# One store and pieced weaving of the turned head outputs, priorities for the state sums, and a wide value projection for five pairs

## The chip, the cores and the metric

The kernel runs on one core of a Trainium2 chip. The metric is the time of one execution on the device in microseconds (us); of several runs the median counts. The core has five engines that work side by side and wait for each other by semaphores: TensorE (PE in the profile, its weight loads PEld) multiplies matrices, VectorE (DVE), ScalarE (ACT) and GpSimd (POOL) work element by element, and SyncE (SP) issues transfers (DMA). Each engine works through its own instructions in the order in which they were written down for it. TensorE writes its results to PSUM, a small memory of eight banks; the other engines read them there.

## The reference

It is one layer of a decoder over 1024 tokens of 1024 features: a normalisation, a token mixer with an output projection and a residual, a second normalisation, an MLP with squared ReLU and a residual, and a last normalisation. The mixer has two branches (RG-LRU and HGRN2), merged by gates. The change lies in the HGRN2 branch and in how its result meets the gates:

```python
proj = h @ w_in
xa, ga, q, f, v, g, m_a, m_b = jnp.split(proj, SPLIT_POINTS, axis=-1)
...
o_inter = jnp.einsum('bhtk,bhkv->bhtv', qc * jnp.exp(cum), state)
...
state = jnp.exp(last)[..., None] * state + jnp.einsum('bhsk,bhsv->bhkv', k_to_end, vc)
...
o = rms_norm(hgrn2_chunkwise(qf, kf, log_f, vf), hg_norm)
y_b = o.reshape(B_, S_, HG_HEADS * HG_DV).astype(h.dtype) * jax.nn.silu(g)
y = jax.nn.sigmoid(m_a) * y_a + jax.nn.sigmoid(m_b) * y_b
return y @ w_out
```

`v` is the value projection, `h` times 1024 columns of `w_in`. `state` is carried from chunk to chunk. `o` holds the head outputs, normalised per head. All of it is float32.

## The kernel before

**Number format.** TensorE multiplies numbers of a shortened float32 (fp32r). To keep float32's accuracy, each operand is split into a high part H (ScalarE's cast, L95 or L121) and a low part L (what is left, VectorE, L99), and each product is made three times, H x H, H x L and L x H, summed in one PSUM bank (`mm3`, L155). The parts of a weight tile of 128 x 1024 lie in tiles with the tag `w`, six at a time. Low parts that are needed a second time are stored in memory (`rest`) and loaded again.

**Stages.** The tokens are cut into two halves of 512 (c = 0, 1) and the heads and channels into four pairs (p = 0 to 3), which gives eight pairs of work, i = 4c + p. Stage i projects `xa`, `q` and `f` of pair i and makes its RG-LRU gates (`pr`, `pi`). It begins with the value projection of the pair before it, i - 1 (`v_of`, `v_steps`; for the first pair another function does it). Between these products TensorE makes the HGRN2 products of pair i - 1 (`hgrn`): scores `sc`, transposes of the scaled keys `pk`, the additions to the state `pkv`, the head outputs `po`. The order of TensorE's instructions is written out: `hgrn` calls `go(n)`, which issues n steps of the stage; `pin` keeps that order. The other engines' orders come from a planner, which goes by the place in the program and by priorities (`tc.high_priority`): a higher one puts an instruction further ahead.

**The value projection.** In `v_steps` (L537) the normalised activations are the stationary operand and the weights the moving one, 256 columns at a time. For each of four groups of 128 tokens and each of eight slices of the features, `mm3` makes three products of 256 columns into the first half of a bank. ScalarE then copies 128 x 256 results to the tile `v` (L551).

**The keys, the state and the outputs.** VectorE scales the keys `kk` in several steps (L694 is a helper that records all multiplications). TensorE transposes them (`pk`, L863), ScalarE copies the result to `kT` (L868), TensorE multiplies by `v` (`pkv`, L873), VectorE makes the four states after each other (`sn`, L884), and TensorE makes the outputs (`po`, L898 and L901).

**Turning.** `on_T` (L558) turns the normalised outputs so that channels come first. The transposing DMA works on units of two bytes, so each float32 falls apart into its two halves, which lie in different rows. `stored` writes them to the memory tensor `od` with two transfers, which put the two halves of one channel beside each other.

**The gates.** After the mixer stages come 14 groups of seven products each (`own`, quads 2 to 15; quad = 4 x pair + gate, gates g, mb, ga, ma). `gate_step(q, step)` makes one of the seven products, 12 matmuls of 512 columns, into the bank X, Y or Z (`gX`, `gY`, `gZ`). For steps 0 to 2 ScalarE copies the bank to a tile `ge` (L1209), for steps 3 to 5 VectorE adds it to one (L1212). `gate_work(q)` applies the gate after a group. At gate 1 of a pair, `with_o(p)` (L1278) loads the turned outputs of the pair from `od` (`op`, L1281), lets ScalarE weave the two halves of each float32 together in one copy of 128 x 4096 units of two bytes (`o`, L1282), and multiplies them into the gate on VectorE (L1285). For the first pair this is called by hand at the end of quad 3 (`own[1]`).

**Queues.** Nearly all loads go through SP's queue in the order of the planner. `in_turn` (L1174) chains some of them one behind the other with a high priority: the weights of quads 2, 3 and 4 and the combined activations `t1`, `n2`, `T3`, `T4` (`gT4L` is the last half of them). The stores of the turned outputs go through ScalarE's queue.

After the gates come the output projection, the MLP and the last normalisation. The change does not touch their work; only the tiles of their weight parts are taken through a new helper.

## Time and profile before

| | |
|---|---|
| runs | 1527.86, 1531.04, 1532.47 us |
| median | 1531.04 us |
| the profiled execution, its own time | 1529.59 us |
| its span | 1527.8 us |
| TensorE, VectorE, ScalarE, GpSimd busy | 99%, 75%, 53%, 10% |
| granted clock of TensorE | 0.999 |
| transfers | 311.01 MB, mean 204 GB/s |
| stores of the turned outputs (od) | 16 of 256 KB |
| loads of the turned outputs (op) | 4 of 1024 KB |

How to read the rows that follow: a row of a timeline has the start and the length in us, the engine and the line, the operation, the tile written and the tiles read, the shape and type, the count, and in square brackets how long the engine was idle before and what ended the idle time. A row of a tile's list has the shortest, median and longest duration in ns. A row of the waits names who waited for whom, then the total in us, the number of times and the longest. A row of the chain of waits has the start, the length and the work. A row of the table by stage has the stretch, its length, the busy time of TensorE, its weight loads, VectorE, ScalarE and GpSimd (each with its count of instructions), the granted clock, the share of the transfer engines and GB/s. A matmul's duration in a row contains its way through the array; what it costs in a dense row of them is the distance of two starts.

### The profile page before, as it was taken

Reading aid. Unit: us, or ns where it says so; the run is one execution under the profiler, and the core shown is the slowest. Engines: PE = TensorE matmul, PEld = TensorE weight load, DVE = VectorE, ACT = ScalarE, POOL = GpSimd, SP = SyncE. Lnnn points to the kernel's source line nnn. Section 1 sums busy time; section 2 is a strip of 40 time slices with the busy share of each in tenths; the row PEclk is TensorE's granted clock in tenths of the full one; section 3 lists DMA queues with packets and bytes.
Section 4 is the critical chain, followed back from the end, with each engine's and each line's share of the span. In section 5 each row is a group of like instructions: output and inputs, shape, how many; then the busy total and the mean of one; then the engine's idle time right before and its main releaser. Section 6 shows DMA issues by size and latency. Waiting matters only on the chain.

```text
span 1527.8 us, 23130 instructions
## 1 busy us (share of the span) xinstructions
PE 1514.5 (99%) x9027; PEld 1268.6 (83%) x9027; DVE 1147.3 (75%) x1661; ACT 811.1 (53%) x1333; POOL 154.5 (10%) x191
## 2 busy tenths in 40 slices
PE   9999999999999999999999999999999999999998
PEld 7888988888889878788888888888888888888886
DVE  6888686485585738786856578888888998888877
ACT  6556746656668336555553447666666722111115
POOL 1021110232633600000000000000000000000000
PEclk9999999999999999999999999999999999999999
DMA  8546456476674384332339334666666766666642
GB/s 298 199 170 217 153 198 221 143 230 220 207 240 158 110 311 156 135 137 87 134 106 331 128 111 161 259 248 251 248 250 249 253 264 264 249 249 250 250 191 110
DMA packets 100047, 311.01 MB, mean 204 GB/s; under 512 B 25313, under 2 KB 38753, under 8 KB 87010
## 3 DMA queue, kind: packets, MB, share of 16 engines
q1 hardware_dynamic: 93392, 298.91, 54.0%
q10 hardware_dynamic: 6546, 10.62, 2.0%
q8 instruction: 71, 1.16, 0.3%
q14 instruction: 38, 0.31, 0.1%
HBM read 201.50 MB, written 103.81 MB: 200 GB/s over the span
## 4 chain that ended last, share of the span: by engine, by line
PE 77%; DVE 4%; DMA 2%; ACT 1%; issue 1%; SPq 0%; DVEq 0%; ACTq 0%
PE uX L158 11%; PE dX L158 11%; PE gX L158 8%; PE po L158 6%; PE dY L158 6%; PE uY L158 6%; PE gY L158 4%; PE pj_f L158 3%; PE pv L158 3%; PE pj_q L158 3%; PE pj_xa L158 3%; PE uZ L158 3%; PE dZ L158 3%; PE gZ L158 2%; PE mb L158 1%
## 5 line engine op out<-in xcount | busy, mean ns | idle before, releaser
L1836 DVE TENSOR_TENSOR acc<-acc,dX 128x512 f32<-128x512 f32 x128 | 85.0, 683 | 26.8 <-PE dX L158 26.1
L95 ACT CAST wA<-q 128x512 fp32r<-128x512 f32 x46 | 28.6, 622 | 118.5 <-PE dX L158 94.4
L99 DVE TENSOR_TENSOR wL<-raw,wH 128x1024 fp32r<-128x1024 f32 x46 | 56.3, 1226 | 33.8 <-ACT wH L95 32.9
L158 PE MATMUL po<-wH,y 128*128 128x512 f32 x256 | 80.5, 391 | 0.0
L95 ACT CAST wH<-raw 128x1024 fp32r<-128x1024 f32 x46 | 48.2, 1049 | 35.1 <-DMA raw<-wts_in 14.8
L1736 POOL TENSOR_TENSOR gx<-acc,gain 128x256 f32<-128x256 f32 x1 | 0.7, 741 | 604.6 <-DVE acc L1836 604.6
L158 PEld LDWEIGHTS po<-wH,y 128*128 128x128 f32 x256 | 48.1, 188 | 9.8
L1836 DVE TENSOR_TENSOR acc<-acc,dY 128x512 f32<-128x512 f32 x64 | 43.6, 685 | 14.3 <-PE dY L158 13.8
L158 PE MATMUL po<-wL,y 128*128 128x512 f32 x128 | 49.8, 389 | 0.0
L1584 ACT ACTIVATE b<-b 128x512 f32<-128x512 f32 x48 | 30.0, 625 | 29.7 <-DVE b L1583 27.9
L158 PE MATMUL uX<-h2B11H,wA 128*128 128x512 f32 x128 | 42.1, 390 | 0.0
L193 POOL TENSOR_TENSOR rstd_h<-rstd_h,mhalf 128x1 f32<-128x1 f32 x8 | 4.3, 543 | 373.0 <-DVE rstd_h L188 373.0
L121 ACT CAST wH<-raw 128x1024 fp32r<-128x1024 f32 x36 | 37.2, 1045 | 7.3 <-issue 3.7
L99 DVE TENSOR_TENSOR wA<-q,wA 128x512 fp32r<-128x512 f32 x46 | 31.4, 685 | 12.8 <-ACT wA L95 12.8
L596 DVE SCALAR_TENSOR_TENSOR xc<-xp,pvt,xc 128x512 f32<-128x512 f32 x48 | 40.0, 841 | 1.2 <-ACT xc L580 1.1
L158 PE MATMUL gX<-hT00H,wA 128*128 128x512 f32 x112 | 36.8, 389 | 0.0
L502 POOL TENSOR_TENSOR stt<-r,stt 128x256 fp32r<-128x256 f32 x16 | 21.2, 1344 | 122.4 <-ACT stt L501 110.2
L1121 DVE TENSOR_TENSOR s<-q,q 128x512 f32<-128x512 f32 x46 | 31.6, 687 | 1.4 <-DMA q<-mlp_in 1.1
L1129 DVE TENSOR_TENSOR s<-q 128x512 f32<-128x512 f32 x46 | 31.5, 685 | 0.2
L905 ACT ACTIVATE on<-po 128x128 f32<-128x128 f32 x64 | 16.8, 277 | 26.1 <-PE po L901 26.0
L1585 ACT ACTIVATE b<-b 128x512 f32<-128x512 f32 x48 | 30.1, 630 | 1.0
L158 PEld LDWEIGHTS uX<-h2B11H,wA 128*128 128x128 f32 x128 | 24.0, 188 | 4.9
(2325 smaller groups left out, 5291.2 us busy)
## 6 DMA issues: line engine op xcount, KB each, us to landing
q<-mlp_in SPq DMA_DIRECT2D x92, 512.0 KB, 3.9
raw<-wts_in SPq DMA_DIRECT2D x80, 512.0 KB, 4.7
rest<-wL SPq DMA_DIRECT2D x36, 512.0 KB, 2.9
wL<-rest SPq DMA_DIRECT2D x36, 512.0 KB, 4.1
hd<-ri SPq DMA_DIRECT2D x16, 256.0 KB, 3.0
od<-onT ACTq DMA_DIRECT2D x16, 256.0 KB, 5.9
cdT<-stT SPq DMA_DIRECT2D x16, 256.0 KB, 3.1
op<-od SPq DMA_DIRECT2D x4, 1024.0 KB, 6.7
```

The costliest lines, as they stand in the source:

```text
L95: ins = casts[name] = A.copy(h, src)
L99: ins = V.tensor_tensor(out=lo, in0=src, in1=h.bitcast(F32), op=ALU.subtract)
L121: A.copy(h, raw)
L158: ins = PE.matmul(o, a, b, start=begins, stop=ends, **how)
L502: G.tensor_tensor(out=lo, in0=src, in1=h.bitcast(F32), op=ALU.subtract)
L596: ins = V.scalar_tensor_tensor(xc[:, s, :], xp[:, j : j + T], pvt[:, PV_CW + 8 * j + u : PV_CW + 8 * j + u + 1], xc[:, s, :], op0=ALU.mult ...
L905: A.activation(row(s, n), halves_of(po[s][:, n * P : (n + 1) * P]), AF.Square, accum_out=ssq[:, 4 * s + n : 4 * s + n + 1],)
L1121: ins = V.tensor_tensor(out=sa[:, 0, :], in0=a21, in1=a22, op=ALU.add)
L1129: V.tensor_tensor(out=sb[:, 0, :], in0=a21, in1=a11, op=ALU.add)
L1584: A.activation(b[:, at, :], b[:, at, :], AF.Relu, scale=-1.0 if at == 2 else 1.0)
L1585: A.activation(b[:, at, :], b[:, at, :], AF.Square)
L1836: return V.tensor_tensor(out=dst, in0=dst, in1=banks[bk, pr], op=op)
```

## The change

- The high and low part of a weight tile become two halves of one tile (`w_pair`); three such tiles take the place of six single ones.
- In `v_steps`, for the pairs with i = 2 to 6, one product of 512 columns (H x H beside H x L, into the two halves of a bank) and one of 256 columns (L x H, into the first half) take the place of three products of 256. ScalarE copies the second half of the bank to `v`, and VectorE adds the first half, with a priority of 400.
- The copies to `kT` and the state sums (L868, L882, L884) get a priority of 100.
- `stored` makes one transfer instead of two, and no longer puts the halves beside each other; the load does that now, with two transfers instead of one (`load_o`).
- The weaving copy is cut into four pieces of 512 tokens. For the pairs 1 to 3 (`spread_o`) the pieces come behind the bank copies of steps 0, 1 and 2 of the next quad, the fourth right after the third, and the product with the gate after step 3. For pair 0 the load joins the chain of `in_turn`, behind `T4`; two pieces each come behind the bank copies of steps 1 and 2 of quad 3, and `with_o(0)` keeps its place with the product alone.

```diff
--- before.py
+++ after.py
@@ -110,9 +110,16 @@
         nc.sync.dma_start(raw, seq[i])
         return raw
 
+    both_parts = {}
+
+    def w_pair(pool, name):
+        t = pool.tile([P, 2, 1024], F32R, tag="w", name=name, bufs=3)
+        both_parts[name] = t
+        return t[:, 0, :], t[:, 1, :]
+
     def split_w(i, raw):
         if i < n_mix + 3:
-            h, lo = (wp.tile([P, 1024], F32R, tag="w", name=f"w{q}{i}", bufs=6) for q in "HL")
+            h, lo = w_pair(wp, f"w{i}")
         else:
             h, lo = (kept[0].tile([P, 1024], F32R, tag=f"k{q}{i - n_mix}", name=f"w{q}{i}") for q in "HL")
         at = pair_tiles[i] if i < len(pair_tiles) else None
@@ -383,7 +390,7 @@
         ws, pv = {}, {}
 
         def w_high(i):
-            ws[i] = tuple(wp.tile([P, 1024], F32R, tag="w", name=f"w{q}{i}", bufs=6) for q in "HL")
+            ws[i] = w_pair(wp, f"w{i}")
             keep(A.copy(ws[i][0], xraws[i]))
 
         def w_low(i):
@@ -536,19 +543,29 @@
 
     def v_steps(c, p, got, between):
         v = mt("v", f"v_{c}{p}", (P, 4, 256))
-        w = [next_w(), next_w()]
+        wide = NPAIR * c + p in (2, 3, 4, 5, 6)
+        w = [(both_parts[f"w{used[0]}"], next_w())[0] for _ in range(2)]
         for tt in range(4):
             pp = bank("sc" if tt == 2 else "pj", f"pv_{c}{p}_{tt}")
             for k in range(8):
                 hh, hl = kt(hT[c], k)
                 cut = slice(tt * P, (tt + 1) * P)
                 cols = slice((k % 4) * 256, (k % 4 + 1) * 256)
-                wh, wl = w[k // 4]
-                mm3(pp[:, :256], hh[:, cut], hl[:, cut], wh[:, cols], wl[:, cols], k == 0, k == 7)
+                both = w[k // 4][:, :, cols]
+                if wide:
+                    pin(PE.matmul(pp.rearrange("p (a b) -> p a b", a=2), hh[:, cut], both, start=k == 0, stop=False))
+                    pin(PE.matmul(pp[:, :256], hl[:, cut], both[:, 0, :], start=False, stop=k == 7))
+                else:
+                    mm3(pp[:, :256], hh[:, cut], hl[:, cut], both[:, 0, :], both[:, 1, :], k == 0, k == 7)
                 if k % 2:
                     if k < 7:
                         yield
-            A.copy(v[:, tt, :], pp[:, :256])
+            if wide:
+                A.copy(v[:, tt, :], pp[:, 256:])
+                with tc.high_priority(400):
+                    V.tensor_tensor(out=v[:, tt, :], in0=pp[:, :256], in1=v[:, tt, :], op=ALU.add)
+            else:
+                A.copy(v[:, tt, :], pp[:, :256])
             between(tt)
             yield
         got["v"] = v
@@ -563,10 +580,7 @@
         turned_on.append(ins)
 
         def stored(dma):
-            for g in range(2):
-                dst = od[p][64 * g : 64 * g + 64, :, 2 * c * T : 2 * (c + 1) * T]
-                src = t[:, 8 * g : 8 * g + 8, :].rearrange("p j x -> p (j x)")
-                dma(dst.rearrange("a h t -> (a h) t"), src)
+            dma(od[p][:, :, 2 * c * T : 2 * (c + 1) * T], t.rearrange("p (g j) x -> p g (j x)", g=2))
 
         return stored
 
@@ -865,7 +879,8 @@
         kTs = mt("rr", f"kT{nm}", (P, 2, 4, P))
         for s, u in both:
             kT.append(kTs[:, s])
-            A.copy(kT[s][:, :nkv, :], pk[s][:, : nkv * P].rearrange("p (n k) -> p n k", n=nkv))
+            with tc.high_priority(100):
+                A.copy(kT[s][:, :nkv, :], pk[s][:, : nkv * P].rearrange("p (n k) -> p n k", n=nkv))
         go(at[3])
         pkv = [bank("hg", f"pkv{c}{u}") for _, u in both]
         for s, _ in both:
@@ -878,17 +893,18 @@
             states.append([scar[:, u, :]] + [sn[:, n, :] for n in range(4)])
             for n in range(nkv):
                 kv = pkv[s][:, n * P : (n + 1) * P]
-                if c == 0 and n == 0:
-                    V.tensor_copy(states[s][1], kv)
-                else:
-                    got["states"] = V.scalar_tensor_tensor(
-                        states[s][n + 1],
-                        states[s][n],
-                        t128[:, 4 * s + n : 4 * s + n + 1],
-                        kv,
-                        op0=ALU.mult,
-                        op1=ALU.add,
-                    )
+                with tc.high_priority(100):
+                    if c == 0 and n == 0:
+                        V.tensor_copy(states[s][1], kv)
+                    else:
+                        got["states"] = V.scalar_tensor_tensor(
+                            states[s][n + 1],
+                            states[s][n],
+                            t128[:, 4 * s + n : 4 * s + n + 1],
+                            kv,
+                            op0=ALU.mult,
+                            op1=ALU.add,
+                        )
         go(at[4])
         po = [bank("hg", f"po{c}{u}") for _, u in both]
         for s, u in both:
@@ -1140,7 +1156,7 @@
                     t = pool.tile([P, 2, 1024], F32R, tag=tag, name=f"w{names[0]}{i}", bufs=bufs)
                     h, lo = t[:, 0], t[:, 1]
                 else:
-                    h, lo = (pools[1].tile([P, 1024], F32R, tag="w", name=f"w{names[0]}{i}{q}", bufs=6) for q in "HL")
+                    h, lo = w_pair(pools[1], f"w{names[0]}{i}")
                 ins = split(src(), h, lo, None, lo_behind, (names[0], i))
                 for j, o in enumerate(names):
                     cols = slice(j * 512, (j + 1) * 512)
@@ -1233,7 +1249,7 @@
         elif gate == 1:
             sigmoids(b, b)
             V.tensor_tensor(out=live["g2"], in0=live["g2"], in1=b, op=ALU.mult)
-            with_o(p)
+            spread_o(q, p)
         elif gate == 2:
             t = gp_tile("sg", f"sg{q}")
             A.activation(t, b, AF.Square)
@@ -1275,18 +1291,46 @@
                     for t, y in enumerate((yh, yl)):
                         nc.sync.dma_start(yd[p][:, t, two, :], y[:, two, :].bitcast(F32))
 
-    def with_o(p):
+    woven, due = {}, {}
+
+    def load_o(p, dma):
         parts, o = gp_tile("ld", f"op{p}"), gp_tile("sg", f"o{p}")
         as_16 = lambda t: t.rearrange("p a b -> p (a b)").bitcast(U16)
-        nc.sync.dma_start(as_16(parts), od[p].rearrange("a h t -> a (h t)"))
-        A.copy(
-            as_16(o).rearrange("p (t h) -> p h t", h=2), as_16(parts).rearrange("p (h t) -> p h t", h=2)
-        )
+        for g in range(2):
+            dma(
+                as_16(parts)[64 * g : 64 * g + 64].rearrange("p (h t) -> p h t", h=2),
+                od[p][:, g, :].rearrange("(a h) t -> a h t", h=2),
+            )
+        woven[p] = o
+
+        def piece(j, behind=None):
+            cut = slice(j * T, (j + 1) * T)
+            ins = A.copy(
+                as_16(o).rearrange("p (t h) -> p h t", h=2)[:, :, cut],
+                as_16(parts).rearrange("p (h t) -> p h t", h=2)[:, :, cut],
+            )
+            if behind is not None:
+                held(ins, behind)
+
+        return piece
+
+    def with_o(p):
         ins = V.scalar_tensor_tensor(
-            live["g2"], live["g2"], pvt[:, PV_HG : PV_HG + 1], o, op0=ALU.mult, op1=ALU.mult
+            live["g2"], live["g2"], pvt[:, PV_HG : PV_HG + 1], woven.pop(p), op0=ALU.mult, op1=ALU.mult
         )
         if p == 0:
             behind_steps(ins)
+
+    def spread_o(q, p):
+        piece = load_o(p, nc.sync.dma_start)
+        for j in range(3):
+            due[q + 1, j] = lambda j=j: piece(j, added[q + 1, j])
+
+        def last():
+            piece(3, added[q + 1, 2])
+            with_o(p)
+
+        due[q + 1, 3] = last
 
     yt = {}
 
@@ -1332,6 +1376,7 @@
     gwork[own[0]]["c"]()
     live["g2"] = gp_tile("b", "g2_0")
     nc.sync.dma_start(live["g2"], g2d)
+    piece = load_o(0, in_turn)
     for q in own:
         n = q + 1
         if n > own[1] and n < QUADS:
@@ -1341,6 +1386,11 @@
                 continue
             pinned[0] = q < own[2]
             gate_step(q, step)
+            if (q, step) in due:
+                due.pop((q, step))()
+            if q == own[1] and step in (1, 2):
+                for j in (2 * step - 2, 2 * step - 1):
+                    piece(j, added[q, step])
             if q == own[0] and step == 4:
                 gate_step(own[1], 0)
             if q == own[2] and step == 4:
```

## The prediction

> **What bounds the kernel now.** I read the page first, then a table by stage, then TensorE's own waits, and last the chain of waits.
>
> ```profile
> span 1527.8 us, 23130 instructions
> ...
> PE 1514.5 (99%) x9027; PEld 1268.6 (83%) x9027; DVE 1147.3 (75%) x1661; ACT 811.1 (53%) x1333; POOL 154.5 (10%) x191
> ```
>
> ```profile
> 20.00:545.00 525.00, 524.32 (x4615) 450.40 (x4614) 373.20 (x656) 324.06 (x645) 143.79 (x164) 1.00 0.58 194
> 545.00:645.00 100.00, 97.41 (x426) 79.42 (x425) 68.88 (x75) 51.27 (x61) 0.00 (x0) 1.00 0.56 199
> 645.00:1515.00 870.00, 869.90 (x3868) 720.18 (x3868) 685.66 (x895) 417.02 (x587) 4.32 (x8) 1.00 0.55 208
> ```
>
> ```profile
> PE gX L158 <- ACT ge L1209: 1.4, 2, 1.0
> PE gX L158 <- DMA gT4L<-cdT: 1.2, 1, 1.2
> ```
>
> The second column of the table after the length is TensorE's busy time. TensorE (PE) is the bound from end to end: from 645 us to 1515 us it misses 0.1 us, in the mixer stages (20 to 545) 0.7 us, and only between 545 and 645 a noticeable 2.6 us. So there are two ways to gain: fewer TensorE cycles, or the few stalls. The sum of the stalls that the change can reach is small, which caps the result from the start.
>
> **The change part by part.**
>
> *Value projection.* The chain of waits shows what a product costs when TensorE runs without a break:
>
> ```profile
> 299.40 11.51 PE pv L158 x96
> ...
> 359.70 11.51 PE pv L158 x96
> ...
> 631.33 3.02 PE gX L158 x12
> 634.34 2.72 PE gZ L158 x12
> ```
>
> The first two rows also give the length of a mixer stage, 60.3 us. A product of 256 columns takes 11.51 / 96 = 119.9 ns, one of 512 columns 2.72 / 12 = 226.7 ns. Column for column both stream alike (256 more columns cost 106.8 ns), so each product carries about 13 ns that don't depend on its width. Before, a step of the projection is three narrow products, 359.7 ns. After, it is one wide and one narrow, 346.6 ns. Five pairs with 4 x 8 steps each are 160 steps: 160 x 13.1 ns = 2.1 us less, 0.42 us in each of five stages. The wide operand is two runs of 256 columns with a gap between them, which the trace has not seen at this width. The nearest rows are the small score products, whose operand is contiguous in one and broken up in the other:
>
> ```profile
> L704 PE MATMUL sc<-q,kk x512: 206/206/230, 81.3 to 500.6; 128*32 128x48 f32 x171
> ...
> L704 PE MATMUL sc<-qa,kb x512: 206/206/230, 85.1 to 504.4; 128*32 128x48 f32 x171
> ```
>
> They are equal, so I charge nothing for the gap. The ends are a gain of 2.1 us and, if the wide product cost as much as two narrow ones (239.8 ns), none. The Trainium skill speaks against this term: "TensorE: Matmul & The Clock Gate", in its section on why a gap is 56 ns and not 53.3, gives warm products N / 2.4 GHz plus about 2.5 ns. By that rule a step would go from 327.5 to 325.0 ns and the term would be an estimated 0.4 us. The trace disagrees: 119.9 and 226.7 ns are both some 13 ns above N / 2.4, so the sum goes by the rows.
>
> *What the wide form adds.* VectorE (DVE) now sums the two halves: 4 additions of 128x256 out of PSUM in each stage, 20 in all, each behind ScalarE's (ACT's) copy. These rows of a stage in steady state, by engine, show the price and the cover:
>
> ```profile
> 367.21 0.41 ACT L551 COPY v<-pv 128x256 f32<-128x256 f32 x1
> ...
> 370.47 1.99 ACT L121 CAST wH<-raw 128x1024 fp32r<-128x1024 f32 x2
> ...
> 373.36 0.91 ACT L551 COPY v<-pv 128x256 f32<-128x256 f32 x3
> ```
>
> ```profile
> 382.17 0.42 DVE L694 TENSOR_TENSOR dd<-sc,mf 128x256 f32<-128x256 f32 x1
> ...
> 384.04 0.44 DVE L723 COPY_PREDICATED dd<-mu,sc 128x192 f32<-128x192 uint8 x1 [0.97 <-PE sc L704]
> 384.77 0.75 DVE L596 SCALAR_TENSOR_TENSOR xc<-xp,pvt,xc 128x512 f32<-128x512 f32 x1 [0.29 <-ACT xc L580]
> ...
> 402.52 0.68 DVE L694 TENSOR_TENSOR kk<-kk,seg 128x512 f32<-128x512 f32 x1
> ```
>
> ```profile
> 403.32 0.49 PE L863 MATMUL pk<-ident,kk 128*128 128x128 f32 x3
> ```
>
> An addition like the one at 382.17 (same shape, one operand in PSUM) takes 0.42 us, so a stage gets 1.7 us of VectorE. TensorE reads the values only after pk at 403.32, 30 us later, so they are not late themselves. What is late is the chain behind them: VectorE has 0.97 + 0.29 = 1.26 us of idle time before it makes kk (the keys scaled for the state), and TensorE's transposes take kk 0.12 us after its end (403.20). TensorE also arrives 0.42 us earlier. If all four additions lie in VectorE's busy stretch, pk waits 1.7 - 1.26 + 0.42 - 0.12 = 0.74 us. If they fall into other idle time, it waits nothing. The other stages with a wide projection, by engine:
>
> ```profile
> 217.47 0.89 DVE L694 TENSOR_TENSOR kk<-kk,seg 128x512 f32<-128x512 f32 x1
> ...
> 275.68 0.69 DVE L694 TENSOR_TENSOR kk<-kk,seg 128x512 f32<-128x512 f32 x1 [1.38 <-PE sc L835]
> ...
> 462.14 0.68 DVE L694 TENSOR_TENSOR kk<-kk,seg 128x512 f32<-128x512 f32 x1
> ```
>
> ```profile
> 218.65 0.60 PE L863 MATMUL pk<-ident,kk 128*128 128x128 f32 x4
> 221.41 0.49 PE L873 MATMUL pkv<-v,kT 128*128 128x128 f32 x2 [0.35 <-ACT kT L868]
> ...
> 279.79 0.38 PE L863 MATMUL pk<-ident,kk 128*128 128x128 f32 x2
> ...
> 463.63 0.38 PE L863 MATMUL pk<-ident,kk 128*128 128x128 f32 x2
> ```
>
> ```profile
> 220.77 1.07 ACT L868 COPY kT<-pk 128x512 f32<-128x512 f32 x2
> ```
>
> The stage with pk at 279.79 has 3.4 us to spare and loses nothing. That at 463.63 has 0.81 us and loses at most 0.05. That at 218.65 has 0.29 us and I found no idle time of VectorE to absorb the additions, so up to 1.7 + 0.42 - 0.29 = 1.8 us; but the wait at 221.41 behind it (0.6 with its refill, below) is then already served, which leaves 1.2. With the 0.74 for the stage shown and for the one before it, taken as alike, the give-back lies between 0 and 1.2 + 2 x 0.74 + 0.05 = 2.7 us. I take 1.2, just under the middle, because the additions go to the head of VectorE's order, ahead of the chain that must not be late.
>
> *Priorities of the state's copies and sums.* The wait at 221.41 is one that they aim at: kT's copies start at 220.77, though pk, eight transposes from 218.65 on at 0.15 us or less each, had ended by 219.9. The other is in the second stage:
>
> ```profile
> 108.45 0.46 PE L898 MATMUL po<-v,scT 128*128 128x128 f32 x2 [0.27 <-DVE sn L884]
> ```
>
> A stall costs more than its idle time, since the products after it must refill the pipeline: the 12 products after the wait at 631.33 took 3.02 us against 2.72, and idle time of 1.0 became 1.3. So 0.27 costs about 0.5 and 0.35 about 0.6. Bounds: 0 to 1.1 us gained. I take 0.5 for the first and 0.3 for the second, which the additions may eat. What is put back is the weight casts on ScalarE and the gate's first operations on VectorE, both with idle time after them (ScalarE is busy 324 of 525 us).
>
> *Weaving in pieces.* The turned head outputs are woven on ScalarE in one copy. Rows by engine:
>
> ```profile
> 578.55 4.84 ACT L1282 COPY o<-op 128x4096 uint16<-128x4096 uint16 x1 [2.13 <-DMA op<-od]
> ...
> 593.22 2.01 ACT L1245 ACTIVATE sg<-sg 128x1024 f32<-128x1024 f32 x2 [2.55 <-DVE sg L1243]
> ...
> 622.05 4.83 ACT L1282 COPY o<-op 128x4096 uint16<-128x4096 uint16 x1 [2.29 <-DMA op<-od]
> ```
>
> ```profile
> 580.51 0.69 DVE L1212 TENSOR_TENSOR gb<-gX,ge 128x512 f32<-128x512 f32 x1 [2.03 <-PE gX L158]
> 583.42 2.35 DVE L1285 SCALAR_TENSOR_TENSOR g<-g,pvt,o 128x2048 f32<-128x2048 f32 x1 [2.21 <-ACT o L1282]
> ```
>
> ```profile
> 597.18 0.50 PE L158 MATMUL gX<-gT3H,ws336H 128*128 128x512 f32 x1 [0.38 <-ACT ge L1209]
> ```
>
> The copy at 622.05 holds ScalarE for 4.83 us, the bank copies queue behind it, and TensorE stalls at 631.33: 1.0 idle, 1.3 us in all. In four pieces of about 1.2 us (4.83 / 4, and somewhat more for four starts), each behind a bank copy, with 2.72 us of products between bank copies, nothing queues: 1.3 us gained. I see no reason for less than 1.0. The first copy (578.55) stalls nobody directly, but VectorE waits 2.21 us for it, and its gate work then runs late: ScalarE waits 2.55 us at 593.22 and TensorE 0.38 us at 597.18, 0.65 with its refill. With the outputs loaded ahead, VectorE's product can start behind the addition at 580.51, some 2.2 us earlier than at 583.42. I take the 0.65; its ends are 0 and 0.8. The third and fourth copies stall nobody (0.1 us is missing after 645).
>
> *Stores and loads.* These are off the path:
>
> ```profile
> L569 ACTq DMA_DIRECT2D od<-onT x16: 326/334/446, 126.6 to 546.4; - x16
> ```
>
> ```profile
> 565.26 3.30 SPq L1176 DMA_DIRECT2D q<-mlp_in x2
> ...
> 570.12 0.42 SPq L1281 DMA_DIRECT2D op<-od x1
> ```
>
> ```profile
> 556.07 10.67 DMA gT4L<-cdT
> ```
>
> Eight stores fewer save 8 x 0.33 = 2.7 us of ScalarE's issue time, spread over 400 us in which it has idle time. The loads double in number (4 issues more on SP's queue, 0.3 to 0.4 us each). The first pair moves from 570.12 to just behind the load of gT4L and ahead of the weights issued at 565.26; those weights are for the next group of seven products, 7 x 2.72 = 19 us away. gT4L itself is on the path (TensorE waits 1.2 us for it), so the load must not overtake it: being issued behind it on the same queue, I charge nothing. If the two shared the engines instead, the bound is the transfer of 1 MB at the 199 GB/s of the row 545:645, 5 us. The paired weight tiles free the high part with the low one: at most one product later, 0.12 us, behind two other tile pairs; nothing.
>
> *The sum.* -2.1 + 1.2 - 0.8 - 1.3 - 0.65 = -3.65 us. The profiled execution took 1529.59 us in all, 1.8 us around its span, so it would take 1525.9. It lies 1.45 us under the median of the runs shown, 1531.04, so I forecast **1527.4 us** for the median.
>
> **The rivals.**
>
> *Everything pays in full.* No give-back, both early waits gone: -2.1 - 1.1 - 1.3 - 0.8 = -5.3, 1525.7 us. For it: VectorE is idle for 152 of the 525 us of the mixer stages. Against it: pk's 0.12 us to spare, twice.
>
> *The additions eat the projection.* Give-back 2.7, only the first of the early waits and the 1.3 and 0.65 gained: -2.1 + 2.7 - 0.5 - 1.95 = -1.85, 1529.2 us. For it: the same 0.12 us, and in the stage at 217.47 no gap that I found.
>
> *VectorE blocks on ScalarE: slower.* VectorE works in the order written down for it. The addition has a high priority, the copy it needs has none: ScalarE made three copies only at 373.36, behind the casts at 370.47, while the last values had been ready since 371.21. If the additions stand where the values are ready, VectorE idles about 2.2 us in each stage with the rest of its chain behind it. It decides once the delay exceeds what pk can spare: then 0.74 + 2.2 = 2.9 us in two stages, 2.2 in that of 463.63, 1.2 + 2.2 = 3.4 in that of 218.65, together 11.5; with -2.1 - 0.5 - 1.95 the total is +6.95, 1538.0 us. Against it: the planner that orders both knows of the copy.
>
> *It doesn't do what it says.* The wide product gains nothing, because the fixed 13 ns turn out to belong to the columns of the broken operand: +2.1 on my sum, 1529.5 us. This is near what the rule of the Trainium skill named above would give (an estimate of 1529.1); the row of 119.9 against 226.7 ns speaks against it.
>
> **How the numbers follow.** The likeliest has 0.50, full pay 0.20, eaten 0.17, blocked 0.06, no gain from width 0.05, a head load that overtakes gT4L (+1.3 at its 5 us) 0.02. The repeats of before spread over 4.6 us, which is 0.3%, about what a measurement of this kernel can tell from no change. The likeliest, with its unknowns, spans 1525 to 1530. Faster by over 0.3% means under 1526.4: about a quarter of the likeliest, and 0.6 of full pay: 0.26. Slower by over 0.3%, over 1535.6, is the blocked case and what I overlooked: 0.09. So 0.65 is left for no difference. The range reaches to full pay with a measurement's spread below it, 1523.8, and above past the eaten case to 1532.4; that leaves out the blocked case.
>
> **What would show it.** In the changed profile a narrow and a wide product of pv should follow each other in 347 ns. TensorE's waits should no longer name ge after 620 us nor kT and sn. If the give-back is real, the waits of pk on kk (or of its weight load) appear near 217, 343 and 403 us, in those stages only. If VectorE blocks, its idle time before the additions names v's copy, 2 us at a time. The forecast is wrong if the stage length of 60.3 us falls by less than 0.1 or more than 0.5 us, or if the wait for gT4L grows past 2 us.

## The result, and the profile after

| on one chip, in turns | runs | median, us | lowest to highest |
|---|---|---|---|
| before | 4 | 1529.89 | 1527.86 to 1532.47 |
| after | 4 | 1547.18 | 1543.63 to 1550.33 |

The ratio is 1.0115, with a 95% interval from 1.0097 to 1.0133: the change costs some 17 us. The profiled execution of after took 1543.63 us, the fastest of its four; its span is 14.0 us longer than that of before. The page of after begins:

```profile
span 1541.8 us, 22779 instructions
...
PE 1516.3 (98%) x8867; PEld 1262.1 (82%) x8867; DVE 1148.5 (74%) x1681; ACT 809.7 (53%) x1345; POOL 155.0 (10%) x191
```

There are 160 matmuls less, as the change says, and yet TensorE is busy for 1.8 us more. The table by stage (stretch, length, busy time of TensorE, its weight loads, VectorE, ScalarE, GpSimd, then the granted clock) shows both reasons:

```profile
20.00:545.00 525.00, 524.68 (x4463) 443.21 (x4462) 375.59 (x676) 324.34 (x645) 144.22 (x164) 1.00 0.59 195
545.00:645.00 100.00, 86.52 (x369) 70.68 (x368) 61.05 (x67) 46.46 (x61) 0.00 (x0) 0.93 0.64 172
645.00:1515.00 870.00, 867.94 (x3858) 717.96 (x3857) 679.59 (x876) 410.41 (x577) 4.33 (x8) 1.00 0.55 207
```

Between 545 and 645 us TensorE misses 13.5 us, where it missed 2.6, and its clock is down to 0.93. Between 645 and 1515 it misses 2.1 us, where it missed 0.1. Times between certain products make this exact. In the table, the mixer goes from the first product of `pr` to the first of the gates, the gates to the first of the output projection, and the last column from the first product `dX` of the MLP's second half to the last of the program:

| us | mixer | gates | to the MLP's second half | from there to the end |
|---|---|---|---|---|
| before | 487.60 | 270.35 | 396.32 | 307.96 |
| after | 485.98 | 283.45 | 396.34 | 310.25 |
| difference | -1.62 | +13.10 | 0 | +2.29 |

TensorE's waits in after name who was late:

```profile
PE gX L165 <- ACT ge L1225: 10.5, 1, 10.5
PE gX L165 <- DMA gT4L<-cdT: 2.9, 1, 2.9
...
PE dX L165 <- DVE acc L1886: 1.2, 1, 1.2
PE dZ L165 <- DVE acc L1886: 0.9, 1, 0.9
PE pk L877 <- DVE kk L708: 0.3, 1, 0.3
```

One wait of 10.5 us for `ge`, ScalarE's copy of a gate bank. The chain of waits (start, length, work) tells what it stood behind:

```profile
539.35 20.52 DMA onT<-on
...
569.93 10.45 DMA gT4L<-cdT
```

`onT<-on` is the last turn of the head outputs, a transposing transfer. It takes 20.52 us. These are ScalarE's rows of that time, first of before, then of after, with what each instruction waited for in brackets:

```profile
541.01 1.59 ACTq L561 DMA_TRANSPOSE onT<-on  x1
...
545.70 0.34 ACTq L569 DMA_DIRECT2D od<-onT  x1
```

```profile
559.89 0.55 ACTq L583 DMA_DIRECT2D od<-onT  x1
560.49 0.60 ACT L1060 ACTIVATE smb<-mb 128x512 f32<-128x512 f32 x1 [14.85 <-DMA onT<-on]
...
562.76 0.59 ACT L1225 COPY ge<-gX 128x512 f32<-128x512 f32 x1 [0.73 <-DVE g L1061]
```

The store to `od` stands in ScalarE's queue behind the turn and waits for its data. Before, it was issued 4.7 us after the turn, after the change 20.5 us. The last sigmoid of the mixer (`smb`) and the first `ge` copies stand behind that store, and TensorE behind them. So the question is why the turn became slow. SP's queue, of before and of after, answers it:

```profile
542.53 0.32 SPq L1176 DMA_DIRECT2D gn2L<-cdn  x1
545.59 0.32 SPq L1176 DMA_DIRECT2D gT3H<-cdT  x1
552.86 0.32 SPq L1176 DMA_DIRECT2D gT3L<-cdT  x1
```

```profile
538.36 0.32 SPq L1192 DMA_DIRECT2D gn2L<-cdn  x1
539.86 0.32 SPq L1192 DMA_DIRECT2D gT3H<-cdT  x1
559.89 0.32 SPq L1192 DMA_DIRECT2D gT3L<-cdT  x1
```

Before, the load of `gT3H` (1 MB) was issued at 545.59, just as the turn had landed. After, it was issued half a microsecond behind the turn's issue and moved beside it. The instruction lists of the two programs show why. Each transfer waits on one of eight completion semaphores (DMAHW0 to 7) that are handed out in rotation, so for the transfer eight places ahead of it. Each transfer that lands adds 16 to its semaphore, so the count says which one is meant. The first two lines of each are in SP's list, the third, the store, in ScalarE's:

```
before
221 L1176 DMA gT3H<-cdT_108 128x2048 [waits DMAHW2_49 to 480]
222 L1176 DMA gT3L<-cdT_108 128x2048 [waits DMAHW3_49 to 480]
527 L569 DMA od_100<-onT_6094 128x1024 [waits DMAHW2_49 to 480]
after
221 L1192 DMA gT3H<-cdT_108 128x2048 [waits DMAHW3_49 to 448, DMAHW2_49 to 464]
222 L1192 DMA gT3L<-cdT_108 128x2048 [waits DMAHW3_49 to 464]
518 L583 DMA od_100<-onT_5871 256x1x1024 [waits DMAHW3_49 to 464]
```

What the store waits on is the turn. Before, the turn was on semaphore 2 of the rotation, and `gT3H`, eight places on, had to wait for the same count: until the turn had landed. One store less shifts everything behind it by one place: now `gT3L` waits for the turn, and `gT3H` goes ahead of it (its 448 on semaphore 3 is an earlier transfer, one lap before the turn's 464). `gn2L` moves by one place as well: before, it waited for the store of the first half of the gate product (`g2d`) and was issued 1.5 us behind the turn; after, it waits for a store that was issued earlier and goes 1.0 us ahead of the turn. Nobody had asked for the old waits, but they protected the turn.

Sorted by size, the packets of the two queues show how the turn loses (the 256-byte ones are the turn's, the 8192-byte ones the loads'; number of packets by when they started, mean time of one):

```
before 542 to 545 us:  2038 of 256 B, 23 ns      10 of 8192 B
after  545 to 548 us:   202 of 256 B, 87 ns      42 of 8192 B, 309 ns
after  554 to 557 us:   352 of 256 B, 155 ns     14 of 8192 B, 310 ns
```

The Trainium skill, "DMA: Bandwidth & Descriptors", section "Queues, rings and completion order", says that each transfer engine goes round the queues that have work and changes at packet borders only. The times agree in kind only: a turn's packet takes four to seven times as long while 8192-byte packets of 309 ns move too. But 14 of those fill 4.3 us of the 48 us that 16 engines have between 554 and 557 us, so taking turns doesn't account for the length. That the turn is slow beside the loads is shown by the runs below; what slows its packets so much stays open.

The stall has a second price. Of the table by stage in smaller steps, and of the products, for after:

```profile
563.00:570.00 7.00, 6.61 (x17) 5.23 (x18) 1.17 (x2) 1.42 (x3) 0.00 (x0) 0.56 0.79 279
```

```profile
564.42 1.05 PE L165 MATMUL gX<-gn2H,ws 128*128 128x512 f32 x2
565.27 0.63 PE L165 MATMUL gX<-gn2L,ws 128*128 128x512 f32 x1
```

For the 7 us behind the stall the granted clock is 0.56, and a product of 512 columns takes (565.27 - 564.42) / 2 = 0.425 us instead of 0.227. A dozen products at 0.2 us more are about 2.5 us. 10.5 + 2.9 + 2.5, less the 2.6 that before lost here, is 13.3, about the 13.1 of the table. The Trainium skill, "TensorE: Matmul & The Clock Gate", section "Wait — 56ns, not 53.3ns?", gives 426.7 ns for 512 columns on the throttled clock; the trace agrees.

### The profile page after: what moved, and what is told of

It reads as the page before. It is cut to its first block, busy times and chain, and to the rows that moved or that the text cites. A ratio compares the mean times of both kernels' runs of the same rounds, so it can differ in the third digit from the quotient of the medians.

```text
span 1541.8 us, 22779 instructions
## 1 busy us (share of the span) xinstructions
PE 1516.3 (98%) x8867; PEld 1262.1 (82%) x8867; DVE 1148.5 (74%) x1681; ACT 809.7 (53%) x1345; POOL 155.0 (10%) x191
## 4 chain that ended last, share of the span: by engine, by line
PE 58%; DVE 3%; DMA 2%; ACT 1%; issue 1%; SPq 0%; ACTq 0%; DVEq 0%
PE dX L165 10%; PE uX L165 10%; PE gX L165 9%; PE po L165 6%; PE dY L165 5%; PE uY L165 5%; PE gY L165 5%; PE dZ L165 3%; PE uZ L165 2%; PE gZ L165 2%; DMA onT<-on 1%; DMA gT4L<-cdT 1%; DVE acc L1886 1%; DVE ws L99 0%; PE xT_h L1482 0%
## 5 line engine op out<-in xcount | busy, mean ns | idle before, releaser
L95 ACT CAST ws<-s 128x1024 fp32r<-128x1024 f32 x92 | 96.3, 1049 | 123.1 <-PE dY L165 53.6
L95 ACT CAST wA<-q 128x512 fp32r<-128x512 f32 (+1 forms) x92 | 76.5, 835 | 127.2 <-PE dX L165 105.6
L99 DVE TENSOR_TENSOR ws<-s,ws 128x1024 fp32r<-128x1024 f32 x92 | 112.2, 1222 | 41.4 <-ACT ws L95 41.3
L99 DVE TENSOR_TENSOR wA<-q,wA 128x512 fp32r<-128x512 f32 (+1 forms) x92 | 87.1, 953 | 39.4 <-ACT wA L95 38.0
L99 DVE TENSOR_TENSOR w<-raw,w 128x1024 fp32r<-128x1024 f32 x41 | 49.8, 1221 | 26.4 <-ACT w L95 26.1
L95 ACT CAST w<-raw 128x1024 fp32r<-128x1024 f32 x41 | 42.5, 1047 | 22.2 <-issue 9.6
L128 ACT CAST w<-raw 128x1024 fp32r<-128x1024 f32 x36 | 37.2, 1045 | 24.0 <-issue 9.1
L165 PE MATMUL gX<-gn2H,ws 128*128 128x512 f32 x112 | 38.7, 408 | 10.5 <-ACT ge L1225 10.5
L165 PE MATMUL uX<-h2T4H,wA 128*128 128x512 f32 x128 | 42.2, 391 | 0.0
L165 PE MATMUL uZ<-h2B21H,wA 128*128 128x512 f32 x128 | 42.1, 390 | 0.0
L165 PE MATMUL uX<-h2n2H,ws 128*128 128x512 f32 x128 | 42.0, 389 | 0.0
L165 PE MATMUL uY<-h2t1H,ws 128*128 128x512 f32 x128 | 42.0, 389 | 0.0
```

Source lines behind the costliest of these rows:

```text
L95: ins = casts[name] = A.copy(h, src)
L99: ins = V.tensor_tensor(out=lo, in0=src, in1=h.bitcast(F32), op=ALU.subtract)
L128: A.copy(h, raw)
L165: ins = PE.matmul(o, a, b, start=begins, stop=ends, **how)
```

## The experiments

Every run stood beside runs of before on the same chip; their medians were 1528.62 (a to d), 1528.64 (e, f, g, i), 1529.2 (h, n, j) and 1528.93 us (p).

### c: before with the one store

```diff
-            for g in range(2):
-                dst = od[p][64 * g : 64 * g + 64, :, 2 * c * T : 2 * (c + 1) * T]
...
+            dma(od[p][:, :, 2 * c * T : 2 * (c + 1) * T], t.rearrange("p (g j) x -> p g (j x)", g=2))
...
-        nc.sync.dma_start(as_16(parts), od[p].rearrange("a h t -> a (h t)"))
+        for g in range(2):
+            nc.sync.dma_start(
...
```

> The kernel before with one store instead of two (and the load in two transfers that the layout then needs); weaving whole, no priorities, no wide projection. Theories 1 and 2: the turn lands some 20 us after its issue and TensorE loses 10 us or more near 560 us: 1541 to 1548 us. Theory 3: 1528 to 1532 us.

Measured: 1547.61 us in one run. The wait and the turn:

```profile
PE gX L158 <- ACT ge L1206: 13.4, 3, 11.8
```

```profile
540.65 21.77 DMA onT<-on
```

As expected. This part alone brings the whole loss, 19.0 us against the median of before beside it. The edit also loads the turned outputs in two transfers; b has these too, and not the loss. The mixer (487.69 us) and the MLP's second half (307.92) are as before; the gates take 18.2 us more.

### b: the change with two stores

```diff
-            dma(od[p][:, :, 2 * c * T : 2 * (c + 1) * T], t.rearrange("p (g j) x -> p g (j x)", g=2))
+            for g in range(2):
+                dst = od[p][:, g, 2 * c * T : 2 * (c + 1) * T]
+                dma(dst, t[:, 8 * g : 8 * g + 8, :].rearrange("p j x -> p (j x)"))
```

> The changed kernel with two stores of the turned outputs in the new layout; all else as changed. Theories 1 and 2: the 10.5 us wait is gone, 1526 to 1531 us; what is left of the change is then -1.6 us in the mixer stages, about -2 us in the gates and +2.4 us of two new waits in the MLP (if those come from the paired weight tiles), so -0.1% give or take 0.1%. Theory 3: 1543 to 1550 us.

Measured: 1533.13 us (10 runs), ratio to before 1.0029 (1.0017 to 1.0041). The turn takes 8.1 us, and no wait for `ge` is left:

```profile
PE gX L165 <- DMA gT4L<-cdT: 2.9, 1, 2.9
...
PE gX L165 <- DMA gT3L<-cdT: 1.5, 1, 1.5
```

So the one store is some 13 of the 17 us (1.0115 against 1.0029). The rest of the change isn't faster than before either: I had expected -0.1%, and it is +0.3%. The mixer keeps its gain (485.81 us), but the gates take 273.03 us, 2.7 more than before, and the end of the MLP 1.7 more, where a wait for `acc` of 0.9 us remains. These two remainders are the subject of n and d.

### a and e: one store, with transfers added behind the turn

```diff
-        nc.scalar.dma_start(g2d[:, 2:4, :], g2[1])
+        for j in range(2):
+            nc.scalar.dma_start(g2d[:, 2 + j, :], g2[1][:, j, :])
```

This is a; e cuts the second half once more. The one store stays. Each added transfer shifts the rotation back by one place.

> The changed kernel, with the last store of the gate product (g2d, second half) cut into two transfers; the turned outputs still leave in one store. Theory 1 (order of completion): in the program each transfer waits for the one issued eight places before it; one transfer less behind the last turning DMA lets the load of gT3H start before the turn has landed, the load's 8 KB packets and the turn's 256 B packets share the engines, the turn takes 20.5 us, and ScalarE stands behind it. With one more transfer behind the turn, gT3H waits for the turn again: the turn lands within 8 us of its issue, TensorE's 10.5 us wait on ge is gone, 1527 to 1532 us. Theory 2 (the single large store itself is slow): nothing changes, 1543 to 1550 us. Theory 3 (the early load and the pieces of the weaving crowd the transfers): nothing changes, 1543 to 1550 us.

> The changed kernel with its single store of the turned outputs, but the last store of the gate half (g2d) cut into three transfers, which shifts the rotation of completion semaphores by two: now the load of gn2L, too, has to wait until the last turn has landed. Theory (the loss is the overlap of the turn with the bulk loads that no longer wait for it): the turn takes 4.5 to 5.5 us instead of 20.5, TensorE waits less than 1 us for ge, the wait for gT4L or gT3L stays (2 to 4 us), and the time is 1530 to 1534 us. Rival 1 (the one store is slow by its own form): the turn is short, but ScalarE still stands behind the store or g2d lands late, waits for ge of several us, 1537 us or more. Rival 2 (the turn is slow for another reason than the loads): it stays at 13 us or more, with a wait for ge of 4 to 10 us, 1537 to 1547 us.

Measured: a 1537.35 us (one run), e 1533.82 (4 runs, ratio 1.0033, 1.0019 to 1.0048). The turns, first of a, then of e:

```profile
539.77 13.01 DMA onT<-on
```

```profile
540.62 8.17 DMA onT<-on
```

Merely cutting another store in pieces takes back half of the loss in a and two thirds in e. So the one store isn't slow by its form; what decides is which loads move beside the turn. In a `gT3H` waited for the turn again, as theory 1 says (it was issued at 552.79 us, the turn landed at 552.78), but its numbers missed: the turn was to land within 8 us and the wait for `ge` to be gone, and 3.8 us of it were left. In e the turn was to take 5 us and took 8.2: with two more transfers `gn2H` also has to wait, for an earlier store, and now falls beside the turn itself:

```profile
539.95 0.32 SPq L1194 DMA_DIRECT2D gn2H<-cdn  x1
548.86 0.32 SPq L1194 DMA_DIRECT2D gn2L<-cdn  x1
```

All profiles together: the turn took 4.6 us where the next load was issued 1.5 us or more behind it (before, d, f, h, p), 7.5 to 8.9 with one load of 1 MB issued between 1.0 us ahead of it and 0.5 us behind it (b, e, g, i, j, n), and 20.5 to 21.8 where both `gn2L` and `gT3H` were issued before it had landed (after, c). a doesn't fit in: `gn2L` alone, issued 0.95 us behind the turn, moved beside it, and it took 13.0 us. That is one execution, and the reason stays open.

### g: two stores and a cut gate store

b with the edit of a.

> The changed kernel with two stores of the turned outputs (the run with two stores took 1533.1 us, its last turn 8.1 us) and the last store of the gate half in two transfers, so that the load of gn2L waits for the landing of the last turn. Theory (the remaining loss between 550 and 600 us comes from the turn that still shares the engines with gn2L): the turn takes 4.5 to 5 us, the waits for gT3L and gT4L fall to 1 to 2 us in all, 1529 to 1531 us. Rival (the combined activations are bound by the transfers themselves, and the mixer's gain of 1.6 us is lost in waiting for them whatever their order): the waits for gT3L and gT4L stay at 3 to 5 us or grow, as gn2L is issued later; 1532 to 1535 us.

Measured: 1533.98 us (5 runs), ratio 1.0035 (1.0022 to 1.0049). The theory wasn't put to the test: the turn still takes 7.5 us, as `gn2H` moved beside it here too (issued at 537.51, the turn at 538.52). The waits for gT3L, gT4L, gT3H and gn2L come to 5.2 us, and waits and time are those of the rival. But it isn't shown that TensorE would wait as long behind a short turn.

### n: the volume behind the turn

```diff
+            cuts = [(2 * c * T, 1024)]
+            if p == NPAIR - 1:
+                cuts = [(0, 1024), (2 * T, 1024)] if c == 0 else [(2 * T, 128)]
+            for at, many in cuts:
...
```

> The changed kernel with two stores, where the two stores behind the last turn write only 128 of 1024 columns each (the rest of that part of od is filled with another stage's data much earlier, so the last pair's second half is left out). The number and order of the transfers there stay as they were, 448 KB of 512 KB less go through the engines. Theory (the mixer's gain of 1.6 us is lost because the loads of the combined activations are bound by the volume that moves between the last turn and gT4L): at some 290 GB/s gT3L and gT4L land 1.5 us earlier against the turn, the waits for gT3L (1.5 us) and gT4L (2.9 us) fall to 2 us or less in all, and the time is 1528 to 1531 us instead of 1533.1. Rival (order and latencies bind, not the volume): the waits stay at 4 to 5 us and the time at 1532 to 1535 us.

Measured: 1529.41 us (10 runs), ratio 0.9999 (0.9988 to 1.0011), beside b's 1.0029.

```profile
PE gX L165 <- DMA gT4L<-cdT: 2.6, 1, 2.6
...
PE gX L165 <- DMA gT3L<-cdT: 0.2, 1, 0.2
```

Counted from the landing of the turn, gT4L landed after 18.9 us instead of 21.2 in b (20.3 and 19.9 in i and j, which have b's transfers), and the waits fell from 4.4 to 2.8 us, a little less than expected; the turn itself took 0.6 us longer. The median fell as forecast, by 3.7 us, more than the shorter waits explain; in the profiled executions the gates take the same (272.95 and 273.03 us), as n's ran longer at half clock. So the volume between the turn and gT4L counts; how much, one profile doesn't settle.

The length of the turn counts as well. In every profile the gates begin 5.2 us after the turn's issue, so a shorter mixer starts the turn earlier too: counted from the first product of `pr`, at 480.66 us in b and 482.44 in before. But in b the turn takes 8.1 us instead of 4.6. It lands 1.7 us later, and so does gT4L (509.90 and 508.17). This is where the mixer's gain goes: TensorE arrives at the gates 1.8 us earlier, and its last load lands 1.7 us later. In both kernels gn2L waits there for the first gate store; in b it was issued 0.5 us behind the turn, in before 1.5. Why that store landed sooner in b, and what the change would take with a turn of 4.6 us, no run shows.

### d: before with the paired weight tiles

```diff
-            h, lo = (wp.tile([P, 1024], F32R, tag="w", name=f"w{q}{i}", bufs=6) for q in "HL")
+            h, lo = w_pair(wp, f"w{i}")
```

The same at the two other places where such tiles are taken.

> The kernel before with the paired weight tiles alone. If the pairs alone bring the two new waits of TensorE on VectorE at the seam to the down projection (1.05 and 1.33 us): 2 to 2.5 us slower than before (+0.15%) with both waits in the profile. If they come from the changed timing ahead of the MLP: no difference (within 0.05%), and no such waits.

Measured: 1533.42 us (6 runs), ratio 1.0032 (1.0017 to 1.0047).

```profile
PE pkv L877 <- ACT kT L872: 0.9, 1, 0.9
PE dZ L162 <- DVE acc L1840: 0.9, 1, 0.9
PE po L902 <- DVE sn L888: 0.6, 1, 0.6
```

I had costed the pairs at nothing, and even the run's expectation, +0.15%, was half of what they cost. The work of the engines is the same, but 384 of 1661 of VectorE's instructions in the trace and 259 of 1333 of ScalarE's stand in another place (by operation, tiles and shape): the planner gives another order. The mixer takes 1.8 us more, the gates 0.9, the end of the MLP 1.8. The waits for `acc` (VectorE has the splits of weights ahead of the additions that free the bank) are in all profiles with pairs and in none without. In the full change the mixer's part is not seen (b: -1.8 us). Why the planner comes to another order isn't settled; four pairs instead of three were not tried.

### h, p and f: the small parts on top of before

h has the pieced weaving and the early load alone, p the priorities alone, f both; stores, tiles and projection are as before.

```diff
 h, f:  -            with_o(p)
        +            spread_o(q, p)
        +    piece = load_o(0, in_turn)
 p, f:  +            with tc.high_priority(100):
```

> The kernel before with only the woven copies in four pieces and the early load of the first pair's outputs (no priorities, two stores, single weight tiles, narrow projection). Theory: the two stalls behind the long copies (597 and 631 us) go, 1.0 to 1.95 us less, and nothing else changes, since the mixer stages are as before; the wait for gT4L stays at 1.2 us; ratio 0.9985 to 0.9995. Rival (what the pieces free is taken back by the early load, which shares the transfer engines with gT4L): the wait for gT4L grows to 2 us or more, ratio 0.9995 to 1.001.

> The kernel before with only the priorities of the copies to kT and the state sums, and the woven copies in four pieces with the early load of the first pair. Two stores, single weight tiles, narrow value projection, and the load of the turned outputs in one transfer, all as before. Theory (the loss of the change comes from the transfers behind the last turn and from the new order that the paired tiles bring): nothing of it here, so the waits at 108 and 221 us (0.6 to 0.8 us with refill) and those at 597 and 631 us (1.95 us) go, 2 to 2.8 us less than before, a ratio of 0.998 to 0.9987. Rival (every shift in the planner's order costs some us, as the paired tiles alone did): new waits of 0.3 to 1 us in gates and MLP, ratio 1.000 to 1.003.

> The kernel before with only the priorities of the copies to kT and the state sums. In the run that had them beside the pieced weaving, the wait at 108 us (0.27 us, 0.4 with its refill) was gone and that at 221 us stood, but TensorE waited 2.6 us for VectorE's qb at 509 us, where VectorE's products of 128x256 took 0.95 us instead of 0.45 while GpSimd worked beside it. Theory (that wait was a chance of one execution, in which GpSimd got in ahead of VectorE; GpSimd's pair of low parts there took 3.65 us instead of 9.2): the profile has no wait for qb of 1 us or more, GpSimd's pair takes 9 us or more, the mixer stages gain 0.4 to 0.5 us, the gates nothing, ratio 0.999 to 1.0002. Rival (the new order of VectorE brings it about each time): the wait for qb of some 2.6 us is there again, the mixer stages take 3 us more and the gates, whose loads are then less late, give 1 us of it back; ratio 1.0005 to 1.002.

| | median, us | runs | ratio | 95% | mixer | gates |
|---|---|---|---|---|---|---|
| h | 1527.25 | 11 | 0.9985 | 0.9976 to 0.9994 | 487.65 | 267.98 |
| f | 1527.70 | 11 | 0.9995 | 0.9984 to 1.0006 | 491.08 | 267.24 |
| p | 1528.64 | 11 | 0.9997 | 0.9987 to 1.0007 | 487.21 | 271.76 |

h is faster than both kernels, as its theory said, by 0.15%, and the only run whose interval lies below 1. f, with 0.9995, lies between its theory and its rival. The gates of h:

```profile
545.00:645.00 100.00, 98.95 (x437) 81.62 (x436) 72.22 (x78) 55.31 (x70) 0.00 (x0) 1.00 0.54 198
```

```profile
PE gX L158 <- DMA gT4L<-cdT: 1.0, 1, 1.0
```

The missing 1.0 us is the wait for gT4L alone. The early load, issued right behind gT4L, did not hold it up (1.2 us before).

In p the stall at 631 us, which has nothing to do with the priorities, took 1.9 us instead of 1.0 and cost clock as well (below). In f the mixer took 3.5 us more, by this wait, which p hasn't:

```profile
PE sc L704 <- DVE qb L694: 2.6, 1, 2.6
```

Up to the gates, VectorE, ScalarE and GpSimd have the same order in f and p, and f's median lies 2.3 us under its profiled execution. So the wait belongs to that execution and not to the priorities, as expected of p, as far as one profile each can tell. The priorities bring 0.4 us in p's mixer (the wait at 108 us), and nothing in the time that can be measured.

### i and j: what the wide product costs

i is b with 512 neighbouring columns as the wide operand. j is b with two steps as wide, wide, narrow, narrow.

```diff
 i:  +                wd = w[k // 4][:, 0, (k % 2) * 512 : (k % 2) * 512 + 512].rearrange("p (a b) -> p a b", a=2)
 j:  +                    narrow = (hl[:, cut], both[:, 0, :]) if k % 2 == 0 else narrow
     +                    if k % 2:
     +                        pin(PE.matmul(pp[:, :256], *narrow, start=False, stop=False))
     +                        pin(PE.matmul(pp[:, :256], hl[:, cut], both[:, 0, :], start=False, stop=k == 7))
```

> The changed kernel with two stores, where the wide product of the value projection takes 512 neighbouring columns of the high part as its moving operand instead of two runs of 256 with a gap of 768 between them. This leaves the product of the high part with the low part of the weights out and computes another matrix in its place, for a look at the cost of the operand's form alone. Theory 1 (the broken operand costs the wide product 9 ns): a step of a wide and a narrow product falls from 352.9 to 346.6 ns or less, and the stage's 32 steps take 11.1 us instead of 11.29. Theory 2 (a change of width or of the PSUM region between products costs it): the step stays at 352 to 354 ns.

> The changed kernel with two stores, where the value projection's products of two steps stand as wide, wide, narrow, narrow instead of wide, narrow, wide, narrow. The sums are the same. Theory (each change of width costs: 236 ns from wide to narrow, 117 back): a wide product in front of a wide one costs 226.7 ns, as in the gates, a narrow one in front of a narrow one 119.9, and two steps take 699.5 ns instead of 705.8. Rival (a product that writes both halves of a bank while the next adds to one of them costs 236 ns whatever follows): two steps take 705 to 709 ns.

The wide products of one stage, of after and i (first and last row quoted; between them lie 14 steps in after, 15 in i):

```profile
297.87 0.39 PE L556 MATMUL pv<-w,hT10H 128*128 128x512 f32 x1
...
302.80 0.40 PE L556 MATMUL pv<-w,hT11H 128*128 128x512 f32 x1
```

```profile
298.48 0.39 PE L557 MATMUL pv<-w,hT10H 128*128 128x512 f32 x1
...
303.77 0.40 PE L557 MATMUL pv<-w,hT11H 128*128 128x512 f32 x1
```

After: 4.93 / 14 = 352 ns a step; i: 5.29 / 15 = 353; j, with 8 double steps from 296.93 to 302.50 us: 5.57 / 16 = 348. The gap in the operand costs nothing, so i's theory 1 fell; i's mixer takes 485.81 us, just as b's (i took 1532.68 us in its one run). Over all steps the distance from a wide product to the next is 236 ns, and from a narrow one 117. In j a wide product costs 233 ns before a wide and before a narrow one alike, a narrow one 116 to 117. So j's sum came near the expected one, but not for the reason given: no form of it reaches the 226.7 ns of the gates' products. Where the 6 to 9 ns come from stays open. j took 1528.99 us in its one run, its mixer 1.0 us less than b's, of which the steps explain 160 x 3.5 ns = 0.56.

## Why the prediction was wrong

I forecast 1527.4 us and a gain of 3.65; it became a loss of 14 in the profiles, 17 in the medians. One rival forecast a loss, 1538.0 us, but because VectorE would stand behind ScalarE's copies; the profile of after has no idle time of VectorE ahead of any of its 20 additions.

**The step that failed** is "Stores and loads. These are off the path", with "eight stores fewer save 8 x 0.33 = 2.7 us of ScalarE's issue time". I counted what the removed transfers cost and looked at where the added ones queue, but not at what the remaining ones wait for. The timeline of before had it in sight: the load of gT3H (545.59) and the store (545.70) were issued within 0.1 us of each other, both on the landing of the turn. After the change the turn took 20.5 us instead of 4.6, and TensorE waited 10.5 us for the copies behind the store. c shows that this step alone makes the loss, a and e that the rotation decides which load goes ahead of the turn, and with it most of the loss.

**The second failed step** is "the paired weight tiles ... nothing": alone they cost 0.3% (d); in the profiles with the whole change the end of the MLP takes 0.9 to 2.3 us more. "One product later, 0.12 us" was right for the tile, but an order that a planner writes answers to small shifts by moving hundreds of instructions.

**The value projection** was mis-sized: 352 ns a step instead of 346.6, so 160 x 7.7 ns = 1.2 us instead of 2.1; the five stages themselves are only 0.17 to 0.19 us shorter each, 0.9 in all. I charged nothing for the gap, which i confirms; what I took from the gates' rows, 226.7 ns for a wide product, does not hold here. The rule of the Trainium skill that I weighed against it gave a gain of 0.4 us, about as far off as mine; its step, 325.0 ns, was further off.

**The give-back** of 1.2 us was not there. No wait for pk appears near 217, 343 or 403 us. I had counted 1.26 us of VectorE's idle time before kk, and stopped too early. Behind those two gaps before has three more, 0.63 us at 398.51 and these:

```profile
400.42 0.75 DVE L673 SCALAR_TENSOR_TENSOR q<-sq,par,pj_q 128x512 f32<-128x512 f32 x1 [0.54 <-ACT sq L671]
401.85 0.75 DVE L673 SCALAR_TENSOR_TENSOR q<-sq,par,pj_q 128x512 f32<-128x512 f32 x1 [0.68 <-ACT sq L671]
```

So there were 3.1 us to absorb the 1.7 us of additions. In after kk is ready 2.4 us ahead of pk, where it was 0.12:

```profile
398.53 0.69 DVE L708 TENSOR_TENSOR kk<-kk,seg 128x512 f32<-128x512 f32 x1
```

```profile
401.61 0.81 PE L877 MATMUL pk<-ident,kk 128*128 128x128 f32 x6
```

The only wait for kk, 0.3 us, stands in a stage with a narrow projection. **The priorities' waits** at 108 and 221 us are gone in after, worth 0.4 and 0.6 us; on top of before (p, f) only that at 108 goes. The mixer's sum, -2.1 + 1.2 - 0.8 = -1.7, met the measured -1.62 by terms that erred against each other. That is luck.

**What the mixer's gain is worth** was the next error. The sum counts it in full. In b TensorE reaches the gates 1.8 us earlier and then waits 3.2 us more for the combined activations, as the turn ahead of them takes 3.5 us more. I read the wait of 1.2 us for gT4L as a danger from the one load that I moved, and not as a sign that whatever delays the turn, or adds volume behind it (n), comes through to TensorE.

**The pieces** were right: -1.3 and -0.65 forecast, -2.37 us in h's gates. In after, the two 4.8 us copies are gone (the first two pieces stand below), and TensorE waits for nothing between 585 and 640 us.

```profile
586.56 2.56 ACT L1308 COPY o<-op 128x1024 uint16<-128x1024 uint16 x2
```

Of the signs I named, the step of 347 ns failed (352), the stage stayed within its bounds (60.13 us, 0.17 less), and the wait for gT4L went past 2 us (2.9), which I had named as a sign against the forecast. None of them looks at the store.

## What to carry to other kernels

Before a transfer is removed or added, list which transfer each later one waits for: where completion semaphores are handed out in rotation, one transfer less moves all these waits by one place, and a small urgent transfer can lose the wait that kept bulk loads away from it. A wait for a transfer on the critical path, even of 1 us, says that whatever delays that transfer, or one that it stands behind, goes into the time: follow its chain back before a gain ahead of it is counted. Change a tile's shape and a priority in separate steps from the work itself, since a planner's new order can cost more than the edit brings.

## What the runs showed of the hardware

**The granted clock changes in steps of 3.41 us, and where a stall falls in them decides what it costs.** In all fourteen profiles the granted clock is 1.00 or 0.50, and any two of its changes in one profile lie a whole multiple of 3.413 us apart. The time at half clock behind a stall is one step in b (567.08 to 570.49 us) and p (631.91 to 635.32), two in n (565.82 to 572.64), four in after (555.50 to 569.15). If a profile is cut along these steps, TensorE's idle time in a step at full clock tells, but for a narrow band, the clock of the next. The row of a step, of b and then of after (TensorE's busy time is the second figure after the stretch):

```profile
563.66:567.08 3.42, 1.00 (x5) 0.50 (x3) 2.33 (x3) 2.48 (x3) 0.00 (x0) 1.00 1.03 305
567.08:570.49 3.41, 2.93 (x7) 2.35 (x8) 1.32 (x2) 0.00 (x0) 0.00 (x0) 0.50 1.03 228
```

```profile
575.98:579.39 3.41, 1.52 (x7) 0.94 (x5) 2.31 (x4) 2.08 (x3) 0.00 (x0) 1.00 1.04 305
579.39:582.81 3.42, 2.38 (x10) 1.97 (x11) 1.84 (x2) 0.40 (x1) 0.00 (x0) 1.00 1.05 217
```

Both kernels wait 2.9 us for gT4L here. In b 2.4 us of it lie in one step, and the next runs at half clock. In after it is split into 1.9 and 1.0 us, and the clock stays. Over all profiles, between 20 and 1500 us, eleven steps at full clock had 1.94 us or more idle (1.94 in p), and each was followed by half clock; none with up to 1.64 us was, and of three with 1.89 to 1.91 us one was. In a step at half clock some eight products of 512 columns take 0.425 us instead of 0.227, so it loses about 1.6 us. A stall of 2 to 3 us costs its own length, and then nothing, or 1.6 us, or in n twice that. The Trainium skill, "TensorE: Matmul & The Clock Gate", section "What's actually happening", gives an idle window of about 3.4 us, which runs freely; the length agrees, but a window with 1.94 us of idle time was enough here.

**What VectorE and GpSimd take beside each other can differ between executions with the same order.** In before and in seven other profiles (after, b, d, h, j, n, p), GpSimd's two subtractions near 495 us take 9.2 to 9.3 us and VectorE's product 0.40 to 0.45; in f it is 3.65 and 0.95. So GpSimd was the faster one there, and VectorE the slower one. Before, then f:

```profile
495.35 9.22 POOL L502 TENSOR_TENSOR stt<-r,stt 128x256 fp32r<-128x256 f32 x2 [18.95 <-ACT stt L501]
```

```profile
494.81 3.65 POOL L502 TENSOR_TENSOR stt<-r,stt 128x256 fp32r<-128x256 f32 x2 [18.93 <-ACT stt L501]
```

```profile
500.35 0.95 DVE L694 TENSOR_TENSOR qb<-qa,seg 128x256 f32<-128x256 f32 x1
```

p has f's order of both engines up to the gates, and takes 9.23 and 0.45 us. The 2.6 us that TensorE then waited in f are of the size of the differences that runs of this kernel show without any change (4.6 us among the four of before). What decides between the two outcomes no run shows.
